# Giving stores out later and moving the retention scores back in a hybrid SGU and retention layer

## The chip, the cores and the metric

The kernel runs on one core of one Trainium2 chip. The metric is the device time of one execution in microseconds (us). The time before is the median of 3 runs, 1109.99 us (1109.15 to 1112.51).

## The reference

One layer of a hybrid decoder is computed for a prompt of 2048 tokens (16 tiles of 128) and a sample of 64 tokens (8 sequences of 8), with a width of 1024:

```python
h = rms_norm(x, norm_pre)
z = h @ w_in                                   # 1024 -> 7 groups of 512
su, sv = gelu(z[:, :512]), gelu(z[:, 512:1024]);  sg = z[:, 1024:1536]
rq, rk, rv, rg = the other four groups         # 4 heads of 128
a_out = silu(sg) * su * (W_s @ layer_norm(sv) + b)      # chunks of 128 positions
q, k = rotary(rq), rotary(rk) * DK ** -0.5
o, s_final = retention(q, k, rv, s0)           # o = (q k^T * decay) v + q S ; S = g S + k^T v
b_out = silu(rg) * group_norm(o)
mix = concat(a_out, b_out) @ w_out
x = x + rms_norm(mix, norm_post)
x = x + sigmoid(x @ w_ple_gate) * (p @ w_ple_proj)
```

## The kernel before

TensorE carries the kernel. Every large product is made with operands that are split into a high and a low part (`A` tiles for activations, `W` tiles for weights), so that one 128x128 by 128x512 block takes three matmuls. These matmuls are called products here. `units` is the list of the work in order: the SGU projections (`Unit` of kind S, 16 tiles and the sample), the projection of `p` (`Ple`, its first half), the retention projections of heads 0 and 1 (`FastR`, called R0 here), the other half of `Ple`, those of heads 2 and 3 (R1), the output projection (kind C, called C1) and the gate (`Fast`, called C2). `FastR` and `Fast` take two tiles at a time with 84 products, by a scheme that needs seven block products in place of eight. For R0 and R1 the sums of activations that the scheme needs are made in the SGU stage (`spill_sums`) and stored to `xsum`, and the sums of weights (`spill_weights`) to `wsum`; both are loaded again later.

The order on every engine is written out by hand. `Stream` counts the products that were issued (`st.count`). Everything else is a generator: it issues some instructions and yields the number of products after which it wants to go on. `st.later(lag, fn)` issues `fn` after `lag` more products. Nothing is put in another order later: each engine's queue, and each queue of DMA issues, takes its instructions in the order in which this program gave them out. An instruction whose data isn't there holds all that stand behind it on that queue. Nearly all loads and stores are issued by SyncE (SP), a few by ScalarE (ACT).

The change touches these names:

- `store` issues a store of one tile `LAG_D` = 12 products after its call; `scatter` issues a transposed tile as four stores, `lag` products after its call and three products apart. `mixT`, `x2T`, `qkT`, `x2d`, `pleD` (`ple` in the rows), `xsum` (`xS..`) and `wsum` (`wT`) are DRAM tiles.
- `r_qk` rotates queries and keys of one tile, stores them transposed to `qkT`, loads them back (line 537) and copies them with ACT to `T` (line 540). The copy is issued `PH_T` = 108 products after the tile's base.
- `r_tile` first makes the state's update (`pu`: lines 622 and, for the last tile, 629), then waits until `PH_S` = 122 products behind its own base, and calls `r_scores`, which waits until the copy `T` has been issued and three more products have passed. The scores are two matmuls of 128x128 that read `T` alone (`s<-t` in the rows); DVE masks them in line 573. The tile's output (`po`) follows at `PH_O`, at least 22 products behind the scores, and `r_norm` with lines 583, 585 and 595 and a scatter to `mixT` with `LAG_M` = 40.
- `sgu_batch` finishes four tiles of the SGU part and scatters them to `mixT`. `Ple.post` copies a result (line 1168) and stores it, half of them from SP and half from ACT. `c1_post` stores `x2d`.
- The loads of `X` for R0 stand in line 1051, their high parts are cast by ACT in line 858, and a finished PSUM bank of `FastR` is copied by ACT in line 933. PSUM has 4 banks for `z` tiles and 4 for `s` tiles.

Of the kernel before, what the change touches and what calls it, by code (L numbers as in the profile page):

```python
# [19 lines left out]
P = 128  # L20
# [16 lines left out]


PH_T = 108
PH_S = 122  # L40
PH_U = 74
PH_O = 146
LAG_L = 14
LAG_O = 30
LAG_D = 12
LAG_M = 40
LAG_W = 14
WARM = 36
F_A = 7
# [58 lines left out]
def hybrid_step(ctx: ExitStack, tc: tile.TileContext, a: dict):  # L108
    nc = tc.nc
    V, S, GP, PE, SY = nc.vector, nc.scalar, nc.gpsimd, nc.tensor, nc.sync  # L110
# [14 lines left out]
    def slot(label, shape, dt=F32):  # L125

        return ring.tile(shape, dt, tag="slot", name=name(label))

    def wtile(shape, dt=F32):
        return slot("W", shape, dt)  # L130
# [4 lines left out]
    def t2k(shape, dt=F32):  # L135
        return slot("t2", shape, dt)

    def t1k(shape, dt=F32):
        return slot("t1", shape, dt)

    def tiny(w):
        return work.tile([P, w], F32, tag="tiny", name=name("ti"), bufs=16)
# [4 lines left out]
    def sbank():  # L147
        return ps_side.tile([P, 512], F32, tag="s", name=name("s"))

    f = lambda ap: ap.bitcast(F32)  # L150
# [18 lines left out]
    mixT = [dram.tile([4 if t < NT else 2, P, KD, 32], F32, name=f"mixT{t}") for t in range(NT + 1)]  # L169
# [4 lines left out]
    wsum = [[{key: dram.tile([P, 512], F32, name=f"w{key}{pr}{k}") for key in ("T1", "T2", "T3", "T4")} for k in range(4)] for pr in range(2)]  # L174
    pleD = [dram.tile([P if t < NT else TS, D], F32, name=f"ple{t}") for t in range(NT + 1)]
    x2d = [dram.tile([P if t < NT else TS, D], F32, name=f"x2d{t}") for t in range(NT + 1)]

    st = Stream()
    np_ = lambda t: TS if t == SAMPLE else P

    def store(dst, src, q=None):
        st.later(LAG_D, lambda: (q or SY).dma_start(out=dst, in_=src))

    def blocks(tile_, src, n):

# [9 lines left out]
    def scatter(dst, src, n, qu=None, lag=LAG_D):  # L195


        def go(q):
            (qu or SY).dma_start(  # L199
                out=dst[q].rearrange("(b c) k r -> c b k r", b=4), in_=src[32 * q : 32 * q + 32]  # L200
            )

        for q in range(n // 32):
            st.later(lag + 3 * q, lambda q=q: go(q))

    def mm(out, l, r, start, stop, again=False):

        st.pe = True
        PE.matmul(out, lhsT=l, rhs=r, start=start, stop=stop, skip_group_check=again)  # L209
# [34 lines left out]

    def fill(steps, counts, lag=LAG_W):
        for (load, high, low), c in zip(steps, counts):
            st.at(c - lag, load)
            st.at(c, high)
            st.at(c + 3, low)

    def spill_weights(pr, k):

        r = {}
        for i in range(2):
            for c in range(2):
                r[i, c] = wtile([P, 512])
                SY.dma_start(out=r[i, c], in_=a["w_in"][4 + 2 * pr - c, 4 * i + k])
        yield 20
        for i, c in ((0, 0), (0, 1), (1, 1), (1, 0)):
            S.mul(out=r[i, c], in_=r[i, c], mul=npre[:, 4 * i + k : 4 * i + k + 1])  # L260
            yield 4
        t1, t2 = wtile([P, 512]), wtile([P, 512])
        for key, out, x, y in (
            ("T1", t1, r[0, 1], r[0, 0]), ("T3", r[0, 1], r[1, 1], r[0, 1]),
            ("T2", t2, r[1, 1], t1), ("T4", r[1, 0], r[1, 0], t2),
        ):
            V.tensor_tensor(out=out, in0=x, in1=y, op=ALU.subtract)
            yield 8
            store(wsum[pr][k][key], out)

    def in_specs(groups):
        return [(g, k, a["w_in"][g, k], npre[:, k : k + 1]) for g in groups for k in range(KD)]
# [175 lines left out]
    def sgu_batch(b):  # L448
        whi, wlo = sgu["w"]
        vh, vl = sbatch.pop(("v", b))  # L450
        us = [sbatch.pop(("u", 2 * b + j)) for j in range(2)]
        for q in range(4):
            ps = sbank().rearrange("p (g t c) -> p g t c", g=2, t=4)
            for j in range(2):
                g = 2 * q + j
                mm(ps[:, j], whi[g // 4][:, g % 4, :], vh[q][:, j], True, False)
                yield 0
                mm(ps[:, j], whi[g // 4][:, g % 4, :], vl[q][:, j], False, False)
                yield 0
                mm(ps[:, j], wlo[g // 4][:, g % 4, :], vh[q][:, j], False, True)  # L460
                yield 0
            yield 1
            for j in range(2):
                g = 2 * q + j
                for h in range(2):
                    u = us[h][g // 4][:, :, 64 * (g % 4) : 64 * (g % 4) + 64]
                    V.scalar_tensor_tensor(
                        out=u, in0=ps[:, j, 2 * h : 2 * h + 2, :], scalar=sbias[:, g : g + 1], in1=u,
                        op0=ALU.add, op1=ALU.mult,
                    )  # L470
        for h in range(2):
            yield 2
            for i in range(2):
                bt = blocks(t2k([P, 512]), [us[h][c][:, i, :] for c in range(2)], P)
                scatter(mixT[4 * b + 2 * h + i][:, :, 0:4, :], bt, P)
                yield 3

    def sgu_sample(uu):
# [97 lines left out]
    def r_norm(t, pr, ps, g):  # L576
# [25 lines left out]
        bt = blocks(t1k([P, 256])[0:n], o.rearrange("p h e -> p (h e)"), n)  # L602
        scatter(mixT[t][:, :, 4 + 2 * pr : 6 + 2 * pr, :], bt, n, lag=LAG_M)

    def r_tile(t, pr, v, g):
# [25 lines left out]
        else:  # L631
            ret["st"] = new
        yield max(0, base + PH_S - st.count)
        yield from r_scores(t, pr, mask[:, 2 * pr : 2 * pr + 2, :])
        T = ret.pop(("T", t, pr))[0]
        yield max(0, max(base + PH_O, ret["scored"] + 22) - st.count)
        s = ret.pop(("S", t, pr))
# [182 lines left out]
    def fast_fill(jobs, counts):  # L820
        for (loads, scales, total, high, low), c in zip(jobs, counts):
            for fn in loads:
                st.at(c - 8 - LAG_W, fn)
            for fn in scales:
# [169 lines left out]
    def spill_sums(j):  # L994

        t0, t1 = 2 * j, 2 * j + 1
        r0, r1 = load_xT(t0), load_xT(t1)
        yield 20
        s2 = slot("sum", [P, 4, P])
        todo = [  # L1000
            ("S1", r1[1], lambda: V.tensor_tensor(out=r1[1], in0=r1[0], in1=r1[1], op=ALU.add)),
            ("S2", s2, lambda: V.tensor_tensor(out=s2, in0=r1[1], in1=r0[0], op=ALU.subtract)),
            ("S4", r0[1], lambda: V.tensor_tensor(out=r0[1], in0=r0[1], in1=s2, op=ALU.subtract)),
            ("S3", r0[0], lambda: V.tensor_tensor(out=r0[0], in0=r0[0], in1=r1[0], op=ALU.subtract)),
        ]
        for key, raw, total in todo:
            total()
            yield 8
            hi, lo = slot("A", [P, 4, P], F32R), slot("A", [P, 4, P], F32R)
            S.copy(out=hi, in_=raw)  # L1010
            yield 8
            V.tensor_tensor(out=lo, in0=raw, in1=f(hi), op=ALU.subtract)
            yield 10
            for o, d in zip((hi, lo), xsum[j][key]):
                store(d, f(o))
            yield 14

    class FastR(Fast):
# [56 lines left out]
    def c1_post(t, part, bank):  # L1075
        src = (yield from result_of(t, bank))[0 : np_(t)]
        n = np_(t)
        if part == 0:
            c1["acc", t] = tiny(2)[0:n]
        acc = c1["acc", t]  # L1080
        c1[part, t] = src
        junk = t2k([P, 512])[0:n]
        S.activation(out=junk, in_=src, func=AF.Square, accum_out=acc[:, part : part + 1])
        if part == 0:
            return
        yield 5
        r = tiny(1)[0:n]
        GP.tensor_tensor(out=r, in0=acc[:, 0:1], in1=acc[:, 1:2], op=ALU.add)
        rms_scale(r, r, n, 1.0 / D)
        yield 6  # L1090
        x2 = [h[0:n] for h in c1.pop(("tok", t))]
        for j in range(2):
            w = t2k([P, 512])[0:n]
            V.scalar_tensor_tensor(
                out=w, in0=c1.pop((j, t)), scalar=r, in1=ret["npost"][j][0:n], op0=ALU.mult, op1=ALU.mult
            )
            yield 3
            V.tensor_tensor(out=x2[j], in0=x2[j], in1=w, op=ALU.add)
            store(x2d[t][:, 512 * j : 512 * j + 512], x2[j])
        yield 12  # L1100
        for j in range(2):
            scatter(x2T[t][:, :, 4 * j : 4 * j + 4, :], blocks(t2k([P, 512])[0:n], x2[j], n), n, (S, SY)[j])
            yield 3


    class Ple:
# [54 lines left out]
        def post(self, t, g, bank):  # L1161
            if self.sample:
                out = yield from result_of(t, bank)
                store(pleD[t][:, 512 * g : 512 * g + 512], out)
                return
            yield 1
            out = slot("P", [P, 512])
            S.copy(out=out, in_=bank)
            store(pleD[t][:, 512 * g : 512 * g + 512], out, (SY, S)[g])


    c2 = {}
# [361 lines left out]
```

## Time and profile before

| | before |
| --- | --- |
| median of 3 runs | 1109.99 us |
| profiled execution, its own time | 1110.83 us |
| its span, first to last instruction | 1108.9 us |
| mean granted TensorE clock | 0.990 |
| PE busy | 1080.3 us |
| DVE busy | 814.1 us |
| ACT busy | 500.9 us |
| mean DMA rate | 229 GB/s |

The profiled execution takes 1.9 us beyond its span. PE is busy in 97% of the span, so that what can be won without fewer products lies in PE's idle time and in the stretches in which its clock was granted at half speed; DVE, the next busiest, has 73%.

### The profile page before, as it was taken

The numbers are of one execution on the slowest core, as the hardware profiler recorded it, in microseconds if no ns is written. First come the engines' busy times: TensorE is split into PE (matmuls) and PEld (weight loads), VectorE is DVE, ScalarE is ACT, GpSimd is POOL, SyncE is SP. The second block draws the span as 40 slices with busy tenths as digits, with TensorE's granted clock in tenths as the row PEclk, the third lists the DMA queues.
The fourth block names the chain that finished last, engine by engine and source line by source line (L and its number), as shares of the span: only waits on it lengthen the run. The fifth ranks groups of instructions, "written<-read, shape, count | busy, mean of one in ns | idle before, by whom it ended". The sixth has DMA issues, their size and how long they took to land.

```text
span 1108.9 us, 16484 instructions
## 1 busy us (share of the span) xinstructions
PE 1080.3 (97%) x5028; PEld 895.3 (81%) x5028; DVE 814.1 (73%) x1504; ACT 500.9 (45%) x1034; POOL 362.9 (33%) x570
## 2 busy tenths in 40 slices
PE   9999999999999999998999999998999999999997
PEld 7888887888777888876788888777788888888886
DVE  4887788786855677879456666766688988886885
ACT  6664554654744244435542333443333243544442
POOL 6765454764301333334113233423455410000000
PEclk9999999999998999999899999989999999999999
DMA  8855868765697678986885566856778787865844
GB/s 306 268 184 157 281 223 257 267 230 174 231 299 253 194 240 281 291 275 207 293 273 180 167 186 196 243 179 198 204 221 247 216 244 221 259 223 190 282 164 142
DMA packets 236344, 253.56 MB, mean 229 GB/s; under 512 B 39776, under 2 KB 141920, under 8 KB 236256
## 3 DMA queue, kind: packets, MB, share of 16 engines
q1 hardware_dynamic: 224448, 243.98, 69.4%
q10 hardware_dynamic: 11808, 8.52, 2.5%
q8 instruction: 40, 0.66, 0.3%
q14 instruction: 48, 0.39, 0.1%
HBM read 172.86 MB, written 79.56 MB: 228 GB/s over the span
## 4 chain that ended last, share of the span: by engine, by line
PE 88%; DMA 4%; DVE 4%; ACT 2%; SPq 1%; issue 1%; POOL 1%; ACTq 0%; POOLq 0%; DVEq 0%
PE z L209 69%; PE s L209 19%; DMA t<-qkT 2%; DMA A<-xS30h 1%; DVE W L236 1%; SPq L199 0%; DMA mixT<-t 0%; DVE C L936 0%; DMA ple<-P 0%; ACT C L933 0%; ACT t L540 0%; DVE C L970 0%; DMA t<-xT 0%; DVE t L191 0%; DVE C L975 0%
## 5 line engine op out<-in xcount | busy, mean ns | idle before, releaser
L209 PE MATMUL z<-W,A 128*128 128x512 f32 x3632 | 899.8, 396 | 9.0 <-ACT C L933 4.4
L209 PEld LDWEIGHTS z<-W,A 128*128 128x128 f32 x3632 | 682.1, 189 | 150.5 <-ACT C L933 5.3
L209 PE MATMUL s<-W,A 128*128 128x512 f32 x672 | 183.6, 405 | 0.0
L209 PEld LDWEIGHTS s<-W,A 128*128 128x128 f32 x672 | 125.4, 190 | 22.0
L933 ACT COPY C<-z 128x512 f32<-128x512 f32 x96 | 56.3, 586 | 151.3 <-PE z L209 147.5
L526 POOL TENSOR_TENSOR t<-t,t 128x256 f32<-128x256 f32 (+1 forms) x34 | 29.7, 872 | 227.5 <-DVE t L523 136.0
L209 PEld LDWEIGHTS s<-t,t 128*128 128x128 f32 (+1 forms) x400 | 73.6, 186 | 12.6 <-issue 3.1
L209 PE MATMUL s<-t,t 128*128 128x128 f32 (+2 forms) x400 | 76.2, 272 | 0.0
L860 DVE TENSOR_TENSOR A<-X,A 128x512 fp32r<-128x512 f32 (+1 forms) x78 | 53.6, 688 | 26.8 <-ACT A L858 26.6
L936 DVE TENSOR_TENSOR C<-z,C 128x512 f32<-128x512 f32 x48 | 33.1, 689 | 47.3 <-ACT C L933 32.1
L238 DVE SCALAR_TENSOR_TENSOR W<-W,c_npre,W 128x512 fp32r<-128x512 f32 x48 | 42.2, 890 | 28.0 <-ACT W L229 23.8
L191 DVE STREAM_TRANSPOSE t<-t 128x512 f32<-128x512 f32 (+3 forms) x69 | 39.3, 572 | 26.3 <-POOL t L527 14.0
L552 ACT ACTIVATE t<-C,rsall 128x128 f32<-128x128 f32 (+1 forms) x68 | 23.7, 395 | 75.2 <-DVE C L936 64.8
L858 ACT CAST A<-X 128x512 fp32r<-128x512 f32 (+1 forms) x78 | 46.9, 603 | 15.9 <-DMA X<-xT 12.1
L377 ACT ACTIVATE t<-t,rsall 128x512 f32<-128x512 f32 (+1 forms) x34 | 24.2, 722 | 47.7 <-DVE t L375 47.7
L1187 ACT ACTIVATE C<-C 128x512 f32<-128x512 f32 (+1 forms) x34 | 21.3, 632 | 53.1 <-DVE C L936 46.2
L236 DVE TENSOR_TENSOR W<-W,W 128x512 fp32r<-128x512 f32 x48 | 34.2, 717 | 14.7 <-ACT W L227 14.6
L287 ACT CAST A<-X 128x512 fp32r<-128x512 f32 (+1 forms) x62 | 37.1, 601 | 16.8 <-DVE t L191 12.2
L419 POOL TENSOR_TENSOR v<-t,v 128x128 fp32r<-128x128 f32 x64 | 36.3, 597 | 18.2 <-ACT v L417 16.7
L600 POOL TENSOR_TENSOR t<-t,t 128x256 f32<-128x256 f32 (+1 forms) x34 | 29.0, 853 | 40.6 <-DVE t L595 17.1
L209 PEld LDWEIGHTS s<-t 128*128 128x128 f32 (+1 forms) x136 | 25.5, 194 | 18.9 <-ACT t L540 14.7
L589 POOL TENSOR_TENSOR ti<-ti,c_cols 128x2 f32<-128x2 f32 (+1 forms) x34 | 9.8, 288 | 94.2 <-DVE ti L585 94.2
(143 smaller groups left out, 1391.2 us busy)
## 6 DMA issues: line engine op xcount, KB each, us to landing
X<-xT SPq DMA_DIRECT2D x106, 256.0 KB, 4.2
W<-w_in SPq DMA_DIRECT2D x80, 256.0 KB, 5.1
X<-x SPq DMA_DIRECT2D x64, 256.0 KB, 4.2
qkT<-t SPq DMA_DIRECT2D x132, 64.0 KB, 2.2
wT<-W SPq DMA_DIRECT2D x32, 256.0 KB, 4.5
W<-wT SPq DMA_DIRECT2D x32, 256.0 KB, 4.3
t<-qkT SPq DMA_DIRECT2D x32, 256.0 KB, 4.6
X<-mixT SPq DMA_DIRECT2D x32, 256.0 KB, 3.5
```

The lines of the kernel that those rows point to most:

```text
L191: V.transpose(out=by_k[:, k : k + nk], in_=part.rearrange("p (k b r) -> p k b r", b=4, r=32))
L209: PE.matmul(out, lhsT=l, rhs=r, start=start, stop=stop, skip_group_check=again)
L236: V.tensor_tensor(out=lo, in0=raw, in1=f(hi), op=ALU.subtract)
L238: V.scalar_tensor_tensor(out=lo, in0=raw, scalar=sc, in1=f(hi), op0=ALU.mult, op1=ALU.subtract)
L287: S.copy(out=hi, in_=r)
L419: GP.tensor_tensor(out=los[q][:, :, t % 4, :], in0=i, in1=f(o), op=ALU.subtract)
L526: GP.tensor_tensor(out=qk[:, :, 0, :], in0=t1[:, :, 0, :], in1=t2[:, :, 1, :], op=ALU.subtract)
L600: GP.tensor_tensor(out=o, in0=o, in1=g.rearrange("p (h e) -> p h e", h=2), op=ALU.mult)
L858: S.copy(out=hi, in_=raw)
L860: V.tensor_tensor(out=lo, in0=raw, in1=f(hi), op=ALU.subtract)
L933: S.copy(out=c[key], in_=banks[b])
L936: V.tensor_tensor(out=c[key], in0=banks[b], in1=c[key], op=ALU.add)
```

## The change

Five kinds of stores are issued later. The sums of `spill_weights` and `spill_sums`, `x2d` in `c1_post` and SP's half of the stores of `Ple.post` get a lag of 26 products (`LAG_S`) in place of 12; the scatter of `sgu_batch` gets 40 (`LAG_M`) in place of 12. In `r_tile` the scores are put at 136 products in place of 122, and the output at 160 in place of 146. No instruction is added or taken away.

```diff
 PH_T = 108
-PH_S = 122
+PH_S = 136
 PH_U = 74
-PH_O = 146
+PH_O = 160
 ...
 LAG_M = 40
+LAG_S = 26
 ...
-    def store(dst, src, q=None):
-        st.later(LAG_D, lambda: (q or SY).dma_start(out=dst, in_=src))
+    def store(dst, src, q=None, lag=LAG_D):
+        st.later(lag, lambda: (q or SY).dma_start(out=dst, in_=src))
 ... spill_weights
-            store(wsum[pr][k][key], out)
+            store(wsum[pr][k][key], out, lag=LAG_S)
 ... sgu_batch
-                scatter(mixT[4 * b + 2 * h + i][:, :, 0:4, :], bt, P)
+                scatter(mixT[4 * b + 2 * h + i][:, :, 0:4, :], bt, P, lag=LAG_M)
 ... spill_sums
-                store(d, f(o))
+                store(d, f(o), lag=LAG_S)
 ... c1_post
-            store(x2d[t][:, 512 * j : 512 * j + 512], x2[j])
+            store(x2d[t][:, 512 * j : 512 * j + 512], x2[j], lag=LAG_S)
 ... Ple.post
-            store(pleD[t][:, 512 * g : 512 * g + 512], out, (SY, S)[g])
+            store(pleD[t][:, 512 * g : 512 * g + 512], out, (SY, S)[g], LAG_S if g == 0 else LAG_D)
```

The first place is SP's queue at the beginning of R0, where the last `sgu_batch` and the first `Ple` units are stored and the first pair of R0 is loaded. `X_3892` is the second of that pair's `X` loads, the one whose cast is a row below. Before:

```order
L1055 DMA A_3806<-xS40l 128x512
L220 DMA W_3817<-w_in 128x512
L199 DMA mixT_104<-t_740_3772 32x4x128 x2
L199 DMA mixT_105<-t_745_3786 32x4x128
L182 DMA ple_228<-P_3793 128x512
...
L182 DMA ple_229<-P_3834 128x512
L199 DMA mixT_106<-t_749_3801 32x4x128
L199 DMA mixT_107<-t_756_3819 32x4x128
L220 DMA W_3887<-w_in 128x512
L199 DMA mixT_107<-t_756_3819 32x4x128
L1051 DMA X_3892<-xT 128x512
```

With the change, from the same load of `xS40l` to the same load of `X` (here `X_3875`):

```order
L1056 DMA A_3805<-xS40l 128x512
L221 DMA W_3816<-w_in 128x512
L183 DMA ple_227<-P_3749 128x512
L221 DMA W_3839<-w_in 128x512
L1056 DMA A_3841<-xS30h 128x512
L1056 DMA A_3842<-xS30l 128x512
L183 DMA ple_228<-P_3792 128x512
L221 DMA W_3871<-w_in 128x512
L1052 DMA X_3875<-xT 128x512
L200 DMA mixT_104<-t_740_3771 32x4x128
```

All sixteen stores of `mixT` stood between the two loads (the "x2" row is two of them), and stand behind the second now, which comes 17 places earlier in the queue.

The second place is PE's queue at the scores of tile 12 of R0 (`s_5877`, read from `T` alone). Before:

```order
L209 MATMUL s_5858<-W_3815,A_5768 128x512
L209 MATMUL s_5858<-W_3826,A_5768 128x512
L209 MATMUL s_5877<-t_1270_5862 128x128
L209 MATMUL s_5858<-W_3815,A_5769 128x512
L209 MATMUL s_5877<-t_1270_5862 128x128
L209 MATMUL s_5858<-W_3844,A_5768 128x512
L209 MATMUL s_5858<-W_3863,A_5768 128x512
```

With the change, from the same product on:

```order
L210 MATMUL s_5860<-W_3814,A_5758 128x512
L210 MATMUL s_5860<-W_3824,A_5758 128x512
L210 MATMUL s_5860<-W_3814,A_5759 128x512
L210 MATMUL s_5860<-W_3837,A_5758 128x512
L210 MATMUL s_5860<-W_3852,A_5758 128x512
L210 MATMUL s_5860<-W_3837,A_5759 128x512
L210 MATMUL s_5887<-t_1271_5864 128x128
L210 MATMUL s_5860<-W_3869,A_5758 128x512
L210 MATMUL s_5887<-t_1271_5864 128x128
```

The scores of this tile come four products later. So it is for tiles 10 to 15 of R0 and of R1 that have an even number, but for tile 12 of R1, where it is seven; the first two tiles of R0 and of R1 move by 14, the others by three to eight. The place of the load of line 537 in SP's queue moves by two places at most.

## Rows read from the trace of the kernel before

**Rows 1.** The page: busy time, share of the span, instructions.

```profile
PE 1080.3 (97%) x5028; PEld 895.3 (81%) x5028; DVE 814.1 (73%) x1504; ACT 500.9 (45%) x1034; POOL 362.9 (33%) x570
```

**Rows 2.** PE's waits: line, what was waited for, us in total, times, longest.

```profile
PE s L209 <- ACT t L540: 12.1, 6, 2.8
PE z L209 <- ACT C L933: 4.4, 2, 4.1
PE z L209 <- ACT P L1168: 2.5, 2, 1.8
```

**Rows 3.** Timeline of PE: start, us, instructions, idle time before them and releaser.

```profile
334.39 5.49 PE L209 MATMUL z<-W,A 128*128 128x512 f32 x12 [4.07 <-ACT C L933]
475.86 0.49 PE L209 MATMUL s<-t 128*128 128x128 f32 x2 [1.33 <-ACT t L540]
500.65 0.49 PE L209 MATMUL s<-t 128*128 128x128 f32 x2 [1.78 <-ACT t L540]
529.25 0.79 PE L209 MATMUL s<-t 128*128 128x128 f32 x2 [1.56 <-ACT t L540]
699.81 0.49 PE L209 MATMUL s<-t 128*128 128x128 f32 x2 [1.94 <-ACT t L540]
733.12 0.80 PE L209 MATMUL s<-t 128*128 128x128 f32 x2 [2.74 <-ACT t L540]
761.55 0.49 PE L209 MATMUL s<-t 128*128 128x128 f32 x2 [2.78 <-ACT t L540]
```

**Rows 4.** Windows of PE: stretch, us, busy (instructions), granted clock, DMA share, GB/s.

```profile
334.40:339.80 5.40, 5.40 (x13) 0.50 0.86 284
339.90:345.30 5.40, 5.40 (x25) 1.00 0.39 132
527.70:534.50 6.80, 5.25 (x15) 0.51 0.69 222
733.20:739.10 5.90, 5.90 (x16) 0.50 1.05 322
```

**Rows 5.** Timeline of PE, two rows that follow each other at full clock.

```profile
492.12 5.61 PE L209 MATMUL z<-W,A 128*128 128x512 f32 x24
497.58 1.29 PE L209 MATMUL s<-W,A 128*128 128x512 f32 x5
```

**Rows 6.** Timeline of ACT before the idle time that ends at 334.39.

```profile
333.23 0.62 ACT L858 CAST A<-X 128x512 fp32r<-128x512 f32 x1 [7.11 <-DMA X<-xT]
333.76 0.58 ACT L933 COPY C<-z 128x512 f32<-128x512 f32 x1
```

**Rows 7.** Timeline of SP's DMA issues around the beginning of R0.

```profile
284.67 0.80 SPq L220 DMA_DIRECT2D W<-wT  x2
296.63 0.32 SPq L182 DMA_DIRECT2D ple<-P  x1
...
329.85 0.43 SPq L1051 DMA_DIRECT2D X<-xT  x1
```

**Rows 8.** All engines, window 400:510: PE, PEld, DVE, ACT, POOL busy, clock, DMA share.

```profile
400.00:510.00 110.00, 106.89 (x543) 90.28 (x542) 83.59 (x184) 50.16 (x101) 35.15 (x54) 1.00 0.91 287
```

**Rows 9.** Waits in SP's queue from 396 to 509 us.

```profile
SPq L199 <- DVE t L191: 6.1, 3, 4.6
...
SPq L182 <- DVE W L267: 2.3, 4, 1.0
```

**Rows 10.** DMA issues of the whole span: count, KB each, us to landing.

```profile
wT<-W SPq DMA_DIRECT2D x32, 256.0 KB, 4.5
...
mixT<-t SPq DMA_DIRECT2D x66, 64.0 KB, 1.8
```

**Rows 11.** Timeline of ACT (a copy of queries and keys) and of DVE (end of R0).

```profile
760.88 0.62 ACT L540 COPY t<-t 128x512 f32<-128x512 f32 x1 [4.72 <-DMA t<-qkT]
...
521.80 0.47 DVE L622 SCALAR_TENSOR_TENSOR t<-t,s 128x128 f32<-128x128 f32 x2
```

**Rows 12.** Timeline of PE: last state matmuls of R0; their update is the DVE row above.

```profile
516.00 0.38 PE L209 MATMUL s<-t,t 128*128 128x128 f32 x2
```

## The prediction

> **What bounds the kernel now.** I read the page's busy times first [rows 1]: PE is busy for 1080.3 of 1108.9 us, DVE for 814.1. So I look for PE's idle time and for stretches at half clock. PE's waits by releaser [rows 2] show that the largest kind, 12.1 us in six waits, ended with the copy of queries and keys (line 540), which the scores read. Another, 4.1 us long, ended with a bank's copy by ACT (line 933). The timeline of PE [rows 3] gives the places: 334.39 for the bank's copy, and six for the scores, three near the end of R0 (475.86, 500.65, 529.25) and three near the end of R1 (699.81, 733.12, 761.55). The windows [rows 4] show what the clock adds: three of the stretches there were granted 0.50 or 0.51, which is 1.2 GHz, and the reader is to see 13 matmuls in the first 5.40 us and 25 in the next 5.40 us, which had the full 2.4 GHz. One product at full clock takes (497.58 - 492.12) / 24 = 0.2275 us [rows 5].
>
> The profiled execution took 1110.83 us, 0.84 us above the median of the three runs, and the sum is made against 1110.83.
>
> **The gap at 334.39.** PE waited 4.07 us for a bank that ACT had not copied. ACT could not: it was held 7.11 us in the cast of line 858 for a load of `X`, and the copy stands behind that cast [rows 6]. That load was issued at 329.85, 3.4 us before the cast began. SP's queue says why so late [rows 7]: after 284.67 + 0.80 the next issue is at 296.63, a store of `ple` whose P wasn't copied; 11.2 us are lost to the queue, and it then runs behind its work. Between the load of `xS40l` and that of `X` lay 16 stores of `mixT`, as SP's order before shows. With the change they lie behind. Each issue of this sort has 0.32 us or more there, so X goes out at least 16 x 0.32 = 5.1 us earlier. By the bytes it is a little less: 16 x 64 KB [rows 10] at 284 GB/s [rows 4] are 3.7 us. The `ple` store, 14 products later, holds SP up to 14 x 0.2275 = 3.2 us less on top. Between 3.7 and more than 5.1 us against a gap of 4.07, I take the whole gap: **-4.07**. With it goes the half speed behind it: (25 - 13) x 0.2275 = **-2.73**. The bound on the other side: the load stays late because SP's lost time sits elsewhere, and 0 is won. The 1 MB of `mixT` stores goes into the stretch from 339.90, where the DMA share is 0.39 [rows 4], so I price it at nothing; without that room it would be the same 3.7 us a little later, on X loads of the next pair.
>
> **The scores.** They are said to go back 14 products. What counts is the order: two tiles of each stage move by 14; the others, because the old place was already ruled by "copy plus three products", move by three to eight, and at five of the six waits by four, at tile 12 of R1 by seven. A score that waited for the copy finds four products (4 x 0.2275 = 0.91 us) in front of it that need nothing from the copy. So each wait shortens by at most 0.91 us, and by 1.59 us at 733.12; the waits (1.33 to 2.78 us [rows 3]) do not vanish. The loads of line 537 hardly move in SP's queue, so nothing else in this part brings the copy forward.
>
> - 475.86, 500.65, 699.81 and 761.55: 4 x 0.91 = **-3.64**. Bounds: 0, if all engines are late together, to the whole of these waits, 7.83, if other edits also free the copy.
> - 529.25: 1.56 us of wait inside a cluster. DVE's update of the last tile's state (line 622) runs at 521.80 [rows 11], its matmuls ended at 516.00 + 0.38 [rows 12]: DVE is 5.4 us behind PE there. What PE wins at this wait it gives back at the next bank. **0** (bounds 0 to -1.56).
> - 733.12: **-1.59**. This gap (2.74) ends in half clock for 5.90 us [rows 4]; there 16 matmuls stand where 5.90 us at full speed would have done twice the work: 2.95 us. A gap of 1.15 us is left, less than that of 475.86 (1.33), and the 110 us around that one were granted 1.00 [rows 8]. So I let the half speed go: **-2.95**, with 0 as the other bound.
>
> **The stores of `wT`, `xS`, `x2d`.** A later store cannot hold SP for an operand that DVE has yet to make: from 396 to 509 such waits (line 182 for line 267) were 2.3 us [rows 9]. What it costs is the distance to the load that reads the data again. For `wT`, 4.5 us from issue to landing [rows 10], the closest load (R1's first sums) comes 8 DMAs behind its store with the change, 15 before; 8 of them are 3.4 us if SP issues one in 0.43 us [rows 7], and 7.3 us if each moves 256 KB at the 287 GB/s of that stretch [rows 8]. Against 4.5 us that is a hold of SP between 0 and 1.1 us, once, near 478 us, where the DMA share is 0.91. It stands against the 2.3 us that SP wins: 0, bounds -1 to +1. The Trainium skill speaks against this part: "DMA: Bandwidth & Descriptors", section "Rules for kernel authors", wants a DMA issued early and its semaphore waited for late. In this trace both sides of the rule exist: the early store of `ple` held the queue 11.2 us [rows 7], so an early issue is only free when its data is there. By the rule this part costs its upper bound and the sum would be about 1 us higher; by the row it costs nothing. `x2d` belongs to C1, and none of PE's waits in [rows 2] ends with a load or a line of that stage, so it is priced at 0; the cover is PE's own work there, and a store held by DVE holds no load that PE is short of.
>
> **Sum.** -4.07 - 2.73 - 3.64 - 1.59 - 2.95 = -14.98; 1110.83 - 14.98 = 1095.9, so **1096 us**. Its own range is 1091 to 1101: 5 us on either side are one half-clock stretch and one gap.
>
> **The rivals.**
>
> *All of it goes.* SP runs up to 14 products further ahead, so that the loads `t<-qkT`, for one of which ACT waited 4.72 us [rows 11], also come sooner. Then the six waits (12.1), 4.07, the two half-clock losses (2.73, 2.95), the two `P` waits (2.5) and the loss in 527.70:534.50 (half of 5.25, 2.6) all go: 26.95, which gives 1084; with a part left, up to 1091. For it speaks that SP was held by DVE's transposes (line 191) three times for 6.1 us [rows 9]; against it that these transposes stay. Chance 0.18.
>
> *Only the gap at 334 closes.* If R0 and R1 are paced by SP's queue or the DMA rings, each wait is lateness that builds up, and a score four products later just waits four products less and the rest is met at the next one. The DMA share of 0.91 from 400 to 510 [rows 8] speaks for that; against it, PE is busy 106.89 of 110 us there. Then 4.07 + 2.73 are won: 1104, with 1101 to 1107 around it. Chance 0.15.
>
> *Nothing is won.* The stall moves: `mixT` stores put in front of another X load give the 6.8 us back, and the scores' 0.91 us go to the next wait. 1107 to 1114, chance 0.05.
>
> *Slower.* Scores and output that come later keep the four side banks for longer while DVE is behind. The order of the change has places where a bank is used again 20 products (4.55 us) after its last matmul; DVE's lag of 5.4 us (521.80 against 516.38) [rows 11, 12] is longer. Each such reuse then costs about 0.9 us, five in a row at one phase end 4.3 us, and a clock that falls some 3 us more. There are three such ends (R0's, and two in R1 near 700 and 750); it decides against the change from 5 us lost per end, against 15 won: 3 x 7 - 15 = +6, 1113 to 1120. Against it: the closest reuse before is 19 to 22 products, no longer. The Trainium skill, "Perfetto Trace Analysis", section "Optimizing Tensor Performance", wants independent matmul groups to rotate through PSUM banks so that one is emptied while the next is computed; no run here shows yet whether four are enough with the scores later. Chance 0.07.
>
> **How the numbers follow.** The forecast (1091 to 1101) has 0.55, the rivals 0.18, 0.15, 0.05 and 0.07. The measurement of this kernel tells about 0.3% (3.3 us) from no change, so faster means below 1106.7: the forecast, the first and nearly all of the second, 0.87; the same 0.06; slower 0.07. The range runs from 1085 to 1107: it leaves out the two last rivals (0.12) and the lower edge of the first.
>
> **What would show it.** Right: no wait of ACT at line 858 near 334 and a granted clock of 1.00 from 334 to 340; the six score waits still there but 0.9 us shorter; a wait near 529 as long as before; the clock near 733 at full speed. Wrong: a wait on `X` a pair later; SP held by loads of `wT` near 478; waits of PE for DVE lines 573, 583 or 595 at the ends of R0 and R1 (the bank's rival); or the six waits gone altogether, with ACT no longer waiting for `qkT` (the first rival).

## The result, and the profile after

The changed kernel takes 1094.46 us (median of 4 runs, 1093.87 to 1096.54); the kernel before, beside it, 1110.93 us. The ratio is 0.9856, with a 95% interval of 0.9834 to 0.9877: 1.4% faster, 16 us. The forecast was 1096 us, with 1091 to 1101 as its own range.

The page of the changed kernel, first part, answers to [rows 1] (every line number from 183 on is one higher than before):

```profile
PE 1074.0 (98%) x5028; PEld 890.4 (82%) x5028; DVE 816.6 (75%) x1504; ACT 499.5 (46%) x1034; POOL 361.1 (33%) x570
```

The span is 1092.0 us. Before, PE was not busy for 1108.9 - 1080.3 = 28.6 us, now for 1092.0 - 1074.0 = 18.0. So 10.6 us came from idle time and 6.3 us from busy time, though PE does the same 5028 instructions: the second part is half clock that is gone (mean granted clock 0.990 before, 0.997 now). The sum of the forecast, split in the same way, was 9.3 us of idle time (4.07 + 3.64 + 1.59) and 5.68 of half clock (2.73 + 2.95). The total and both parts fit. Where they came from fits less well.

PE's waits after (against [rows 2]):

```profile
PE z L210 <- ACT P L1169: 3.9, 3, 1.5
PE s L210 <- ACT t L541: 3.7, 3, 2.0
...
PE s L210 <- POOL t L528: 0.6, 1, 0.6
```

The wait for the bank's copy is off the list, and the scores wait 3.7 us in place of 12.1. The timeline of PE shows the places (against [rows 3]):

```profile
513.70 1.65 PE L210 MATMUL z<-W,A 128*128 128x512 f32 x6 [1.47 <-ACT P L1169]
516.29 1.91 PE L210 MATMUL z<-W,A 128*128 128x512 f32 x7 [0.94 <-ACT P L1169]
518.82 0.49 PE L210 MATMUL s<-t 128*128 128x128 f32 x2 [0.62 <-ACT t L541]
536.75 8.61 PE L210 MATMUL z<-W,A 128*128 128x512 f32 x35 [1.49 <-ACT P L1169]
...
708.63 0.49 PE L210 MATMUL s<-t,t 128*128 128x128 f32 x2 [0.65 <-POOL t L528]
719.72 0.49 PE L210 MATMUL s<-t 128*128 128x128 f32 x2 [1.05 <-ACT t L541]
727.73 0.63 PE L210 MATMUL s<-t 128*128 128x128 f32 x2 [2.04 <-ACT t L541]
```

Of the six waits of the scores, four have no row any more (tiles 10 and 12 of R0, 10 and 14 of R1), 1.56 became 0.62, and tile 12 of R1 keeps 1.05 of 2.74. The last row is new: it is tile 13 of R1, which did not wait before. The windows of PE (stretch, us, busy, clock, DMA share, GB/s):

```profile
328.00:333.40 5.40, 5.40 (x25) 1.00 0.54 136
400.00:510.00 110.00, 109.76 (x561) 1.00 0.88 275
513.00:520.00 7.00, 4.74 (x20) 1.00 0.49 160
...
727.70:733.10 5.40, 5.37 (x23) 0.68 0.05 20
```

The stretch behind the old gap of 334 has 25 matmuls in 5.40 us, as many as the stretch at 2.4 GHz in [rows 4]; before it had 13. The end of R0 no longer falls to half clock, though it still idles (4.74 of 7.00 us busy). The only place left with a lower clock is the one behind tile 13's new wait. And from 400 to 510, where the rival saw the DMA rings as the pace, PE is busy for 109.76 us in place of 106.89 at a DMA share of 0.88.

SP and ACT at the old gap (timeline, against [rows 6, 7]):

```profile
320.73 0.90 SPq L1052 DMA_DIRECT2D X<-xT  x1
321.72 0.43 SPq L200 DMA_DIRECT2D mixT<-t  x1
```

```profile
328.03 0.59 ACT L934 COPY C<-z 128x512 f32<-128x512 f32 x1 [1.00 <-PE z L210]
336.25 0.62 ACT L859 CAST A<-X 128x512 fp32r<-128x512 f32 x1 [6.50 <-DMA X<-xT]
336.78 0.58 ACT L934 COPY C<-z 128x512 f32<-128x512 f32 x1
```

`X` goes out 9.1 us earlier (320.73 against 329.85). ACT copies the bank when PE is done with it, and then waits for a later `X` nearly as long as before, 6.50 us. That `X` now has moved `mixT` stores ahead of it. A bank's copy stands right behind this cast too (336.78), but PE never waits for that one.

### The profile page after: what moved, and what is told of

Read it like the earlier page. It is cut to its first block, busy times and chain, and to the rows that moved or that the text cites. A ratio compares the mean times of both kernels' runs of the same rounds, so it can differ in the third digit from the quotient of the medians.

```text
span 1092.0 us, 16478 instructions
## 1 busy us (share of the span) xinstructions
PE 1074.0 (98%) x5028; PEld 890.4 (82%) x5028; DVE 816.6 (75%) x1504; ACT 499.5 (46%) x1034; POOL 361.1 (33%) x570
## 4 chain that ended last, share of the span: by engine, by line
PE 90%; DVE 3%; DMA 3%; ACT 2%; issue 1%; SPq 1%; POOL 1%; ACTq 0%; DVEq 0%; POOLq 0%
PE z L210 71%; PE s L210 19%; DMA t<-qkT 1%; DVE W L237 1%; DVE C L937 1%; DMA wT<-W 1%; SPq L200 1%; DMA mixT<-t 0%; ACT P L1169 0%; DMA t<-xT 0%; ACT W L228 0%; ACT t L541 0%; DVE W L239 0%; ACT C L934 0%; DMA W<-wT 0%
## 5 line engine op out<-in xcount | busy, mean ns | idle before, releaser
L210 PE MATMUL s<-W,A 128*128 128x512 f32 x672 | 174.8, 398 | 0.0
L861 DVE TENSOR_TENSOR A<-X,A 128x512 fp32r<-128x512 f32 (+1 forms) x78 | 55.1, 707 | 21.8 <-ACT A L859 19.2
L192 DVE STREAM_TRANSPOSE t<-t 128x256 f32<-128x256 f32 (+3 forms) x69 | 39.6, 574 | 24.7 <-POOL t L601 12.8
L420 POOL TENSOR_TENSOR v<-t,v 128x128 fp32r<-128x128 f32 x64 | 37.0, 606 | 20.4 <-ACT v L418 20.4
L1084 ACT ACTIVATE t<-z 128x512 f32<-128x512 f32 x32 | 19.1, 596 | 47.4 <-PE z L210 45.5
L601 POOL TENSOR_TENSOR t<-t,t 128x256 f32<-128x256 f32 (+1 forms) x34 | 31.5, 928 | 27.0 <-DVE t L596 16.3
```

The lines of the kernel that those rows point to most:

```text
L192: V.transpose(out=by_k[:, k : k + nk], in_=part.rearrange("p (k b r) -> p k b r", b=4, r=32))
L420: GP.tensor_tensor(out=los[q][:, :, t % 4, :], in0=i, in1=f(o), op=ALU.subtract)
L601: GP.tensor_tensor(out=o, in0=o, in1=g.rearrange("p (h e) -> p h e", h=2), op=ALU.mult)
```

## The experiments

All run beside the kernel before; the median of that was 1112.35 us in the first two sets and 1111.72 us in the third.

**Set 1: the parts apart.** The kernel *scores_alone* has only this of the change:

```diff
-PH_S = 122
+PH_S = 136
-PH_O = 146
+PH_O = 160
```

> Only the scores and the output are moved (122 to 136, 146 to 160); all stores stand as before. Theory A (the sum of the prediction): the gap near 334 stays at 4 us with its half clock; the six waits of the scores shorten by 0.9 us each (1.6 at the last but one) and the half clock there goes: 8 us won, near 1102.5 us. Theory B (the waits went because SP runs freer, not because the scores come later): the waits stay or come back at the next tile, 0 to 2 us won, 1109 to 1111. Theory C (all of the score waits went by the move): 12 us won, near 1098.

Measured: 1102.15 us, ratio 0.9905 (0.9876 to 0.9933). The time is what theory A said, but the waits are what theory C said: in its trace the same four waits have no row, the three that are left are those of the changed kernel, the half clock at the end of R0 and near the old 733 is gone, and the gap at 334 is there with 5.31 us and its half clock. So the moved scores and outputs did more than shorten each wait by its four products, and the bigger gap at 334 and the new wait took some of it back.

*stores_alone* has all the later stores and the old `PH_S` and `PH_O`; *mixt_alone* has of the stores only

```diff
-                scatter(mixT[4 * b + 2 * h + i][:, :, 0:4, :], bt, P)
+                scatter(mixT[4 * b + 2 * h + i][:, :, 0:4, :], bt, P, lag=LAG_M)
```

and *lag_s_alone* only the `LAG_S` of `wsum`, `xsum`, `x2d` and `ple`.

> Only the stores are given out later; scores and output stand as before. Theory A: the gap near 334 goes (-6.8 us), the six waits of the scores stay as they were: near 1104 us. Theory B: the loads of queries and keys come earlier too, and most of the waits shrink: 1096 to 1099. Theory C as A: 1104.

> Only the scatter of the SGU batch to mixT is given out 40 in place of 12 products later. Theory A: these 16 stores alone stood in front of the load of X, so this alone closes the gap near 334: -6.8 us, near 1104. Rival: what held SP was the store of ple, which waits for its copy; the gap then shrinks by 3 to 4 us at most and may keep its half clock, 1106 to 1110.

> Only the stores of the sums of weights and activations, of x2d and SP's half of ple are given out 26 in place of 12 products later. Theory A: no change on PE, 1109 to 1112, but for up to 3 us at the gap near 334, since ple holds SP less. Rival (B): freeing SP's queue from waits for DVE brings the loads of R0 and R1 forward, the waits of the scores in R0 shrink by 3 us or more: 1104 to 1107.

Measured: *stores_alone* 1106.74 us, 0.9946 (0.9927 to 0.9965); *mixt_alone* 1102.85, 0.9911 (0.988 to 0.9942); *lag_s_alone* 1111.76, 0.9988 (0.9968 to 1.0008). In the first two the gap near 334 is gone with its half clock; in the third it has 3.33 us and the half clock. So moving the 16 `mixT` stores alone closes it, and the store of `ple` that holds SP had little to do with it: with its lag of 26 products in the changed kernel it still goes out at 297.03 (before 296.63).

All stores together look no better than `mixT` alone. Two places of each trace bear on this. Timeline of PE and windows, *stores_alone*:

```profile
470.65 0.49 PE L210 MATMUL s<-t 128*128 128x128 f32 x2 [2.46 <-ACT t L541]
...
727.70 0.80 PE L210 MATMUL s<-t 128*128 128x128 f32 x2 [3.36 <-ACT t L541]
```

```profile
470.60:475.40 4.80, 4.75 (x16) 0.64 1.08 366
727.70:733.10 5.40, 5.40 (x15) 0.50 1.00 302
```

The same tiles in *mixt_alone*:

```profile
469.81 0.49 PE L210 MATMUL s<-t 128*128 128x128 f32 x2 [1.17 <-ACT t L541]
...
725.82 0.49 PE L210 MATMUL s<-t 128*128 128x128 f32 x2 [3.22 <-ACT t L541]
```

```profile
469.80:475.20 5.40, 5.39 (x26) 1.00 1.05 355
725.80:731.20 5.40, 5.38 (x26) 1.00 0.93 257
```

Two stretches at a lower clock separate these two executions; the number of waits does not (five waits of the scores with 11.8 us in *stores_alone*, seven with 10.3 in *mixt_alone*). They took 1105.36 and 1100.00 us; the kernels themselves are not shown to be apart, since their intervals overlap. Theory A had all six waits stay: tile 12 of R0 does not wait in either trace, though neither scores nor outputs were moved.

The hold that the forecast had named, on a sum of weights that was stored too shortly before, exists in *stores_alone* and, with 1.2 us, in *lag_s_alone*. Waits in SP's queue, *stores_alone*:

```profile
SPq L221 <- DMA wT<-W: 1.3, 1, 1.3
```

The forecast had 0 to 1.1 us for it. The load that it held goes out at 475.47, behind the wait of tile 10 that ended at 470.65, so it is not why that wait is longer than in *mixt_alone*; that stays open. In the traces in which the scores were moved too, this hold is at most 0.3 us.

**Set 2: scores and outputs apart, and two variants.** *outputs_alone* leaves the scores (0 to 2 products off) and gives the outputs 28 products behind them, *scores_only* moves the scores and keeps the outputs near their old place:

```diff
 outputs_alone: PH_S = 122, PH_O = 146
-        yield max(0, max(base + PH_O, ret["scored"] + 22) - st.count)
+        yield max(0, max(base + PH_O, ret["scored"] + 28) - st.count)
 scores_only: PH_S = 136, PH_O = 146
-        yield max(0, max(base + PH_O, ret["scored"] + 22) - st.count)
+        yield max(0, max(base + PH_O, ret["scored"] + 16) - st.count)
```

> All stores and the scores stand as in the kernel before (scores within one or two products), the outputs come 6 to 8 products later behind them. Theory D (the waits that the forecast left over went because the output's work on DVE and its stores on SP no longer stand in front of the next copy): the waits at tile 12 of R0 and at tiles 10 and 14 of R1 shrink by about 1 us or more each, those at tile 10 of R0 and tile 12 of R1 stay; 3 to 6 us won, 1105 to 1109 beside 1111. Theory A (the score's own place does it): nothing won, 1110 to 1112.

> All stores stand as before, the scores come 3 to 5 products later (2 at tile 12 of R1, 7 at tile 14), and the outputs stand where they were (within 4 products, mostly earlier). Theory A: each wait shrinks by what its scores moved, 0.7 to 1.1 us; 4 to 8 us won, 1103 to 1107. Theory D: waits at tile 10 of R0 shrink by that, but tile 12 of R0 and tile 10 of R1 keep 0.7 us or more, and the half clock at the end of R0 and near tile 12 of R1 stays: 3 to 4 us won, 1107 to 1108.

Measured: *outputs_alone* 1112.58 us, 1.0001 (0.9984 to 1.0019); *scores_only* 1103.63, 0.9922 (0.9896 to 0.9948). The timeline of PE of *outputs_alone*, waits of the scores:

```profile
479.95 0.49 PE L210 MATMUL s<-t 128*128 128x128 f32 x2 [2.17 <-ACT t L541]
...
701.09 0.49 PE L210 MATMUL s<-t 128*128 128x128 f32 x2 [0.93 <-ACT t L541]
710.07 0.80 PE L210 MATMUL s<-t 128*128 128x128 f32 x2 [2.80 <-ACT t L541]
738.33 0.49 PE L210 MATMUL s<-t 128*128 128x128 f32 x2 [1.59 <-ACT t L541]
747.48 0.80 PE L210 MATMUL s<-t 128*128 128x128 f32 x2 [2.96 <-ACT t L541]
```

In time the outputs alone win nothing, where theory D wanted 3 to 6 us. The waits of tile 12 of R0 and tile 14 of R1 are gone and that of tile 10 of R1 is halved (1.94 to 0.93), as theory D said; but tiles 11 and 13 of R1 wait in their stead, tile 10 of R0 waits longer (1.33 to 2.17), and behind these three waits the clock is lower.

*scores_only* is theory A in time: it wins 8.7 of the 10.2 us of *scores_alone*, and the intervals overlap. Only the lower clock behind the gap at 334 is left in its trace; the half clock at the end of R0 and near 733, which theory D wanted to stay, is gone with the scores alone (PE busy 1075.8 us, 1080.3 before). Its waits fit neither theory:

```profile
480.07 0.49 PE L210 MATMUL s<-t 128*128 128x128 f32 x2 [1.59 <-ACT t L541]
...
706.24 0.49 PE L210 MATMUL s<-t 128*128 128x128 f32 x2 [0.50 <-ACT t L541]
```

Tile 10 of R0 waits 1.59 us, more than before. Tile 12 of R0 keeps 0.57 of 1.78 and tile 14 of R1 1.26 of 2.78, where its scores were moved by seven products. Tile 10 of R1 has no row, but tile 11 (706.24) has a new one. The waits of the scores add up to 8.1 us here and to 3.7 in *scores_alone*, where the outputs were moved too.

How the outputs can shorten a wait is seen at tile 12 of R0. In SP's queue the load of that tile's queries and keys stands behind the stores of the next tile's, and these come from DVE: it sums a bank (`C<-z`), rotates the result and transposes it. DVE before, first and last steps:

```profile
481.57 0.69 DVE L936 TENSOR_TENSOR C<-z,C 128x512 f32<-128x512 f32 x1 [1.19 <-ACT C L933]
...
487.20 0.73 DVE L595 TENSOR_SCALAR t<-s,ti,ti 128x128 f32<-128x128 f32 x2 [1.34 <-POOL ti L591]
487.84 0.70 DVE L191 STREAM_TRANSPOSE t<-t 128x512 f32<-128x512 f32 x1
```

and in *outputs_alone*:

```profile
487.10 0.69 DVE L937 TENSOR_TENSOR C<-z,C 128x512 f32<-128x512 f32 x1 [3.98 <-ACT C L934]
...
491.97 0.69 DVE L192 STREAM_TRANSPOSE t<-t 128x512 f32<-128x512 f32 x1
493.54 0.73 DVE L596 TENSOR_SCALAR t<-s,ti,ti 128x128 f32<-128x128 f32 x2 [0.87 <-POOL ti L592]
```

The transposes stood behind the output's scaling (L595), and stand ahead of it now. From the bank's sum to the transposes it takes 4.9 us in place of 6.3, and to ACT's copy (499.98 before, 502.31 here) 15.2 in place of 18.4. PE arrives at the scores (504.57) 17.5 us behind the bank's sum, as before (17.3, without its wait). The stores can do the same: in *mixt_alone* DVE's order is the old one, but the load comes 11.5 us behind the bank's sum in place of 13.1, and the wait is gone as well.

Tile 14 of R1 is another matter, though DVE's order changed there too. The bank's sum before and in *outputs_alone*:

```profile
741.44 0.69 DVE L936 TENSOR_TENSOR C<-z,C 128x512 f32<-128x512 f32 x1 [4.35 <-ACT C L933]
```

```profile
743.37 0.69 DVE L937 TENSOR_TENSOR C<-z,C 128x512 f32<-128x512 f32 x1 [1.78 <-ACT C L934]
```

From there to the copy it takes 19.4 us before and 19.8 in *outputs_alone* and in the changed kernel (723.62 to 743.37): the copy comes no sooner. It is PE that comes later, 17.3 us behind the bank's sum before, 22.1 in *outputs_alone* (765.49) and 22.0 in the changed kernel (745.59), because it was held in between, at tile 13, by a wait of 2.96 or 2.04 us and the lower clock behind it. Where the clock behind tile 13 stayed high, the copy came after 19.2 us (*scores_alone*) or 17.8 (*after_again*, in set 3), and PE after 20.4 in both. So the wait of tile 14 went mainly because PE was held at tile 13.

*later_scores* and *mixt_scores* start from the changed kernel:

```diff
 later_scores
-        ret["T", t, pr] = (T, st.count + 3)
+        ret["T", t, pr] = (T, st.count + 14)
 mixt_scores
-LAG_S = 26
+LAG_S = 12
```

> As the changed kernel, but the scores wait until 14 products have passed since the copy, in place of 3, so that they stand 10 to 11 products behind their place before. Theory A: the waits that are left (near 519, 720 and 728 us, 3.7 us in all, with a stretch of half clock worth about 2 us) go: 1089 to 1091 beside 1094.5. Rival (banks): the side banks are held longer, PE waits for DVE at the ends of R0 and R1 instead: 1094 to 1100.

> As the changed kernel, but wsum, xsum, x2d and ple are stored 12 products behind as before; only the scatter of the SGU batch and the scores and outputs are moved. Theory A: those stores are worth nothing on PE, 1093 to 1096, with the bit that ple gives at the gap near 334 not needed. Rival (from the two runs with and without them, 1106.7 against 1102.9): they cost 3 to 4 us, and this kernel runs at 1090 to 1092.

Measured: *later_scores* 1094.04 us, 0.983 (0.9801 to 0.9859); *mixt_scores* 1096.58, 0.986 (0.9829 to 0.9891). The second is the changed kernel's ratio: the four `LAG_S` stores are worth nothing beside the rest. The first loses the waits at tiles 12 and 13 of R1, as theory A said, but misses its 1089 to 1091 us: it gains waits at tile 15 of R0 (1.57 us), at tile 14 of R1 and at 546. Timeline of PE, *later_scores*:

```profile
545.81 10.11 PE L210 MATMUL z<-W,A 128*128 128x512 f32 x36 [3.97 <-ACT C L934]
...
747.03 0.49 PE L210 MATMUL s<-t 128*128 128x128 f32 x2 [1.12 <-ACT t L541]
```

It is not the banks' rival (no wait for DVE's lines 574, 584 or 596): ACT holds the copy of a bank at the start of the second half of `Ple`. What ACT did there is in its timeline:

```profile
544.75 0.33 ACTq L183 DMA_DIRECT2D ple<-P  x1
545.17 0.59 ACT L934 COPY C<-z 128x512 f32<-128x512 f32 x1 [3.22 <-DMA W<-w_in]
```

The copy reads only the bank. Right ahead of it ACT issues a store of `ple` itself (ACT's half of them, which the change leaves at 12 products), and that store did not go out before 544.75. So ACT stood at this store and not at the copy; the profile puts the wait down to a load of `W`, and what the store waited for is not shown.

**Set 3: the result again, and what is left.** *after_again* is the changed kernel; *mixt_later* is *later_scores* with `LAG_S` at 12; *later_8* has `st.count + 8` in place of `+ 14`.

> The changed kernel itself, beside the two that follow: 1094 to 1097, with the waits of its profile (near 719 and 727 us, half clock behind the second) again. If its gaps lie elsewhere this time, they are a matter of when transfers land and not of the order.

> Only the scatter of the SGU batch, the scores (14 products behind the copy) and the outputs moved; wsum, xsum, x2d and ple stored as before. If the gap of 4 us near 546 us comes from the order that the later scores make on SP and ACT, it is here as well: 1094 to 1097. If it was made together with the later stores of ple, it goes and 4 to 6 us are won: 1088 to 1091.

> As the changed kernel, but the scores wait for 8 products behind the copy. Theory A: the three waits that are left by the scores shrink by about what the scores move, and nothing else changes: 1091 to 1094. Rival (what is won at one score is met at the next place that the same late copy or load holds): 1094 to 1097.

Measured: *after_again* 1095.51 us, 0.9853 (0.9829 to 0.9876); *mixt_later* 1093.04, 0.9822 (0.9797 to 0.9847); *later_8* 1093.40, 0.9834 (0.9809 to 0.9858). *mixt_later* has the gap near 546 again (4.22 us), with ACT's store of `ple` at 544.98 ahead of the copy, so it comes with the later scores and not with the later stores of SP. *later_8* splits it: 1.31 us there, 0.56 and 0.67 us at tiles 12 and 13 of R1, and 2.16 at tile 14; its time is theory A's, its waits are the rival's. All three medians lie below the changed kernel's, by 2.5 us at most, and the intervals overlap: no better version is shown. *after_again* has its waits at the same tiles, 0.82 and 2.04 us, and 1.24 us at tile 10 of R0, which the first profile did not have, beside smaller ones. Behind its 2.04 us the clock stayed at 2.4 GHz:

```profile
730.50:735.90 5.40, 5.40 (x30) 1.00 0.06 20
```

## Why the prediction was right, and where it was not

- **The gap at 334.39** (-4.07 and -2.73): right in mechanism and size. *mixt_alone* closes it alone, and PE's products run 6.8 us ahead from there in the changed kernel. Three details were off. `X` came 9.1 us earlier, not 5.1: the 16 issues took 7.8 us of SP before, 0.49 each and not 0.32. The `ple` store's lag, which the step counted on top with up to 3.2 us, moved nothing: SP got past the first of them no sooner (297.03, 296.63 before), though more loads now go out ahead of it. In *lag_s_alone* the gap was 0.74 us shorter than before, less than it differs between kernels with the same stores. And ACT does wait at line 858 (now 859) near 334, for a later `X`, but PE does not wait for the copy behind it.
- **Four waits at 0.91 us each** (-3.64): mis-sized. They measured 1.33 + 1.78 + 1.94 + 2.78 = 7.83, the bound that the text gave for "other edits also free the copy". The step that failed is "nothing else in this part brings the copy forward", together with taking each wait by itself. At tile 12 of R0 the outputs' new place brings the copy forward, and so do the stores, each alone; at tile 10 of R1 *outputs_alone* halves the wait with DVE's order changed in the same way. At tile 14 of R1 the copy came up to 1.7 us sooner in one profile of the changed kernel and no sooner in the other; in both, the scores' four products and the hold of PE at tile 13 cover the wait, and that hold is counted against the change below. For tile 10 of R0 no help was found; its wait is 0 to 1.24 us in the two profiles of the changed kernel, around the 0.42 that the forecast left.
- **529.25** (0): right for the idle time. The cluster idled 0.70 + 0.66 + 1.80 + 1.56 = 4.7 us before and 1.47 + 0.94 + 0.62 + 1.49 = 4.5 after. But the half clock at 527.70, which the forecast let stand, went, as in the first rival: 2.6 us. *scores_alone* and *scores_only* have that too.
- **733.12** (-1.59 and -2.95): the first is right at its place (2.74 to 1.05, -1.69), and the half clock there went. But part of it came back one tile later. Before, 9.3 us lay between the scores of tile 12 and those of tile 13, with half clock in them, and ACT's copy for tile 13 was ready; in the changed kernel PE is there after 6.0 us, ahead of the copy, and waits 2.04 us. In the first profile the clock fell there too (23 matmuls in 5.37 us, where *after_again* has 30), and it took PE 17.9 us from tile 13 to tile 14, against 16.3 in *after_again*: 1.6 us. So 3.6 of the 4.6 us came back in the first profile, 2.0 in *after_again*. The forecast asked of no other stall what is late next, and should have asked it here.
- **Stores of wT, xS, x2d** (0): right. The hold for `wT` exists, 1.3 us where the forecast bound it by 1.1, but only with the old scores; *mixt_scores* shows the lag to be worth nothing. The rule of the Trainium skill ("DMA: Bandwidth & Descriptors", section "Rules for kernel authors") to issue a DMA early and wait for it late was right for that one load, with 1.3 us, and did not decide.
- **The rivals.** "Only the gap at 334 closes" is out: *scores_alone* wins 10 us without it. "Slower" is out: no row has PE waiting for DVE to empty a side bank, even in *later_scores*. "All of it goes" came nearest in R0, where most waits and the half clock went, but not by its mechanism alone: of the score waits the stores alone remove only that of tile 12 of R0.

That the total came out within 2 us is in part luck. Two errors cancelled: 4.2 us more at four waits and 2.6 us at the end of R0, against 3.6 us that came back at tile 13, 0.65 us of a new wait for POOL, and small ones. What stays open is what sets the size of the gap at 334 where it exists: it was 4.07, 3.33, 5.31, 5.17 and 7.41 us in five kernels with the same 16 stores ahead of the load, and in all but the second SP's order up to there is that of the kernel before. Each is one profiled execution. Also open is what holds ACT's own store of `ple` at 545 in *later_scores*.

## What to carry to other kernels

A store that stands ahead of a load in one queue costs what the load is late for, so look first for the stores between a hold of the queue and the next load that a busy engine needs. When work is moved back, list what stands behind it on every engine, not only on the one that waits: here the outputs' work on DVE, three steps away from PE, told on how soon one tile's queries were copied. Moving it won no time alone, so such a step is to be measured and not only argued. And when a stall is removed, ask of the very next consumer whether the stall was what let it be on time; about half to three quarters of the gain of one place was lost 8 us later. A wait that has gone from one place is not won until PE's next waits have been read.

## What was not expected of the hardware

Whether the granted clock falls to half behind an idle stretch of PE did not follow its length. It fell after 2.46 us in *stores_alone* (16 matmuls in 4.75 us) and after 2.04 us in the changed kernel, and stayed at full speed after 3.22 us in *mixt_alone* and after 2.04 us at the same tile in *after_again*. Such a fall cost 1.6 us at tile 13 in the changed kernel and 2.7 us behind 334 before, more than half of the wait ahead of it, so two profiles of one program can differ by that.
